# Stick-breaking attention in a hybrid decoder trunk: key sums as matmuls, or as a running sum along the free axis

## The chip, the cores and the metric

The kernel runs on 1 core of one Trainium2 chip. The metric is the device time of one execution in microseconds (us); the time before is the median of three runs.

## The reference

A trunk of two layers works on 512 tokens of width 1024 in fp32: a SwiGLU half-step, a mixer, a cross-attention over 256 memory rows, and a second half-step. The mixer has eight stick-breaking heads of width 64 beside four gated delta-rule heads of width 128, and one output projection over both. The change lies in the stick-breaking heads, for each block of 128 queries:

```python
z = jnp.einsum('bhtd,bhsd->bhts', qb, kb, preferred_element_type=F32) * scale
causal = s_idx < t_idx
log_beta = jax.nn.log_sigmoid(z)
log_1m_beta = jnp.where(causal, log_beta - z, 0.0)
between = lax.cumsum(log_1m_beta, axis=3, reverse=True) - log_1m_beta
a = jnp.where(causal, jnp.exp(log_beta + between), 0.0)
outs.append(jnp.einsum('bhts,bhsd->bhtd', a.astype(v.dtype), vb))
```

With softplus(z) = -log(1 - sigmoid(z)), the weight of key s for query t is exp(z minus the sum of softplus(z) over the keys from s up to t). That sum over the keys is what the change computes in another way. Keys at or after the query get a large negative score.

## The kernel before, in words

Activations lie with features on the 128 partitions and tokens along the free axis. Every fp32 product is made of fp32r parts: an operand is split into a high part (a cast on ACT, `split_act`, L164) and a low part (a subtraction on DVE, `split_low`, L169), and `mm3` (L194) adds three matmuls. All matmuls go through `mm` (L118), transposes through `transpose` (L496). Weights come in units of 128x1024 (`load`, L175, on the SP queue), are split ahead, and `products` (L199) issues eight slices of three matmuls per unit.

TensorE's order is written by hand, the other engines' order is found by the compiler's scheduler. `weave` (L92) runs generators as threads on a virtual clock that counts matmul time: a thread yields a number of virtual ns to wait, or names of marks; whoever comes first in the list and is due goes on. In the mixer (L912) the threads are, in this order: the row norms, the delta-rule heads one after the other (`gdn_head`, L728, with high priority), the four pairs of stick-breaking heads (`sb_pair`, L583), and the projections (`mixer_dense`, L948), which fill the rest. When no thread is due, the virtual clock jumps; the chip waits for data alone.

A delta-rule head (L728 to L903) makes transposes and decays, then five small levels (L809 to L822: a transpose and a mask multiply on DVE, a product, a subtraction), two wide levels (L839 to L850), and a loop over four chunks of three dependent products (L858 to L888). A head's projections need the mark `q` of the head two before; the out-projection's first two pairs of blocks (`project_out`, L449) may begin before the delta-rule heads are done, but wait for the mark `sb3` of the last stick-breaking pair, which is set 17600 virtual ns after its output; then come the turned and gated delta-rule outputs (`gated`, L983).

A stick-breaking pair makes, for each of two heads j: scores (L610) with keys on the partitions, in three groups `SBB` of a PSUM bank each, for key block s all queries from that block on (widths 512, 384, 256 and 128): a mask matmul and two products; softplus from Abs, Exp, Ln on ACT (L621 to L623) and a DVE operation (L624), then a split into two parts. `sums` (L630) subtracts from each score the softplus of all keys behind it, by matmuls with a negative triangle and negative ones (`cr`): for each s and each s2 >= s two matmuls, 20 a head. `weights` (L639) takes the exponential (L642) and splits again; `values` (L645) multiplies by the padded values into bank `av`. L681 copies the result, L683 to L697 norm it.

Of the kernel before, what the change touches and what calls it, by code (L numbers as in the profile page):

```python
# [52 lines left out]
class Trunk:  # L53
# [67 lines left out]
    def setup(self):  # L121
# [23 lines left out]
        self.cr = self.sb([P, 2, P], "cr", F32R)  # L145
        self.cb = self.sb([P, 3, P], "cb", BF16)
        self.ntri, self.nones = (self.cr[:, i, :] for i in range(2))
        self.nsb, self.ngd, self.idb = (self.cb[:, i, :] for i in range(3))
        nc.gpsimd.tensor_copy(self.ntri, stage[:, 0:P])
        nc.gpsimd.tensor_scalar(out=self.nones, in0=self.ones, scalar1=-1.0, scalar2=None, op0=ALU.mult)  # L150
# [430 lines left out]
    SBB = (((2, 0, 256),), ((1, 0, 384), (3, 384, 128)), ((0, 0, 512),))  # L581

    def sb_pair(self, layer, pair):  # L583
        nc = self.nc
        mm = self.mm
        t1s = ("s15", "s16", "s17")
        names = [f"s{i}" for i in range(19, 27)]
# [9 lines left out]
        zs, sp, aa = {}, {}, {}  # L597
        av = None

        def split(t, w):  # L600
            if w <= S // 2:
                one = self.slot(self.turn("sbs", names), F32R)
                hi, lo = one[:, :w], one[:, w:2 * w]
            else:
                hi, lo = (self.slot(self.turn("sbs", names), F32R)[:, :w] for _ in range(2))
            self.split_act(hi, t)
            self.split_low(lo, t, hi)
            return hi, lo

        def scores(j, n):  # L610
            bl = self.SBB[n]
            z = zs[j, n] = self.bank("at", self.AT)
            w = sum(b[2] for b in bl)
            for i, (s, c, width) in enumerate(bl):
                mm(z[:, c:c + P], self.idb, self.nsb, start=i == 0, stop=False, skip_group_check=True)
                ks = slice(s * P, (s + 1) * P)
                mm(z[:, c:c + width], kk[j][:, ks], qq[j][:, s * P:], start=False, stop=False, skip_group_check=True)
                mm(z[:, c:c + width], kk[j][:, ks], ql[j][:, s * P:], start=False, stop=True, skip_group_check=True)
                yield 200.0
            t1 = self.slot(self.turn("t1", t1s))[:, :w]  # L620
            nc.scalar.activation(t1, z[:, :w], AF.Abs)  # L621
            nc.scalar.activation(t1, t1, AF.Exp, scale=-1.0)
            nc.scalar.activation(t1, t1, AF.Ln, bias=1.0)  # L623
            nc.vector.scalar_tensor_tensor(out=t1, in0=z[:, :w], scalar=0.0, in1=t1,  # L624
                                           op0=ALU.max, op1=ALU.add)
            hi, lo = split(t1, w)
            for s, c, width in bl:
                sp[j, s] = (hi[:, c:c + width], lo[:, c:c + width])

        def sums(j, n):  # L630
            bl, z = self.SBB[n], zs[j, n]
            for s, c, width in bl:
                for s2 in range(s, NT):
                    for part in sp[j, s2]:
                        mm(z[:, c + (s2 - s) * P:c + width], self.ntri if s2 == s else self.nones, part,
                           start=False, stop=True, skip_group_check=True)
                    yield 0

        def weights(j, n):  # L639
            w = sum(b[2] for b in self.SBB[n])  # L640
            a = self.slot(self.turn("t1", t1s))[:, :w]
            nc.scalar.activation(a, zs[j, n][:, :w], AF.Exp)  # L642
            aa[j, n] = split(a, w)

        def values(j, n):  # L645
            hi, lo = aa[j, n]
            for i, (s, c, width) in enumerate(self.SBB[n]):
# [10 lines left out]
        for j in range(2):  # L658
# [11 lines left out]
            if j == 0:  # L670
                yield from scores(1, 1)
# [596 lines left out]
```

## Time and profile before

| | |
|---|---|
| median of 3 runs | 2524.72 us (2523.73 to 2525.19) |
| profiled execution | 2528.47 us |
| its span, first to last instruction | 2526.7 us |
| mean granted TensorE clock | 0.996 of full speed |
| layer 0's mixer, from its first projection to its last block | about 365 to 740 us |
| layer 1's mixer | about 1620 to 2000 us |

Rows give engine, line, operation, output<-inputs by the program's names, shapes and how often. PE is TensorE, PEld its weight loads, DVE VectorE, ACT ScalarE, POOL GpSimd. Timelines give start and duration in us; a burst is merged into one row with its count, and its duration ends with the modelled end of its last matmul, which overlaps the next row. In brackets stands idle time of the engine before the row and what ended it.

### The profile page before, as it was taken

How to read it: one execution, taken by the hardware profiler on the slowest of the kernel's cores; microseconds unless marked ns; L12 is line 12 of the kernel's file. 1: busy time of each engine (PE TensorE's matmuls, PEld its weight loads, DVE VectorE, ACT ScalarE, POOL GpSimd, SP SyncE). 2: the span in 40 equal slices, each digit the busy share in tenths (PEclk: the TensorE clock that was granted, in tenths of full speed). 3: DMA queues.
4: the chain of work that ended last, by engine and by line, in shares of the span. 5: the costliest groups of instructions: out<-in, count | busy, mean ns of one | idle time of the engine just before them, and what ended most of it. 6: DMA issues, size and time to landing. Idle time of an engine off the chain costs nothing.

```text
span 2526.7 us, 30844 instructions
## 1 busy us (share of the span) xinstructions
PE 2469.2 (98%) x12268; PEld 2070.6 (82%) x12268; DVE 1438.3 (57%) x2585; ACT 970.7 (38%) x1545; POOL 10.5 (0%) x21
## 2 busy tenths in 40 slices
PE   8999999999999999999999999999999999999997
PEld 6888887888889888888888888778888988888886
DVE  6443467788675563444554443687876755544345
ACT  4222236555544432222322222466555444322222
POOL 0000000000000000000000000000000000000000
PEclk9999999999999999999999999999999999999999
DMA  5223232111233123332323222311111432322322
GB/s 192 84 100 100 98 94 67 42 51 36 66 110 125 59 92 100 100 101 88 101 95 98 97 89 94 98 59 42 51 43 51 150 101 67 100 85 99 100 94 65
DMA packets 64672, 220.16 MB, mean 87 GB/s; under 512 B 7312, under 2 KB 9616, under 8 KB 64528
## 3 DMA queue, kind: packets, MB, share of 16 engines
q1 hardware_dynamic: 64096, 217.15, 26.5%
q8 instruction: 96, 1.57, 0.3%
q10 hardware_dynamic: 432, 1.04, 0.1%
q14 instruction: 48, 0.39, 0.0%
HBM read 216.07 MB, written 2.10 MB: 86 GB/s over the span
## 4 chain that ended last, share of the span: by engine, by line
PE 89%; DVE 8%; ACT 1%; issue 1%; DMA 0%; DVEq 0%; SPq 0%; ACTq 0%
PE b L118 88%; DVE wlo L169 2%; PE b L496 1%; DVE s L169 1%; ACT whi L164 1%; DVE qkv L713 1%; DVE s L624 0%; DVE s L810 0%; DVE qk L169 0%; DMA wraw<-f1i 0%; DVE s L822 0%; ACT s L164 0%; DVE s L835 0%; DVE s L836 0%; DVE s L429 0%
## 5 line engine op out<-in xcount | busy, mean ns | idle before, releaser
L118 PE MATMUL b<-xh,whi 128*128 128x512 f32 x2112 | 843.6, 399 | 10.1 <-ACT whi L164 8.4
L118 PE MATMUL b<-xh,wlo 128*128 128x512 f32 x2112 | 826.3, 391 | 0.0
L118 PE MATMUL b<-xl,whi 128*128 128x512 f32 x2112 | 825.7, 391 | 0.2
L164 ACT CAST whi<-wraw 128x1024 fp32r<-128x1024 f32 (+1 forms) x408 | 407.9, 1033 | 1033.5 <-PE b L118 947.6
L118 PE MATMUL b<-s,whi 128*128 128x512 f32 (+1 forms) x2136 | 591.6, 364 | 0.2 <-ACT whi L164 0.2
L169 DVE TENSOR_TENSOR wlo<-wraw,whi 128x1024 fp32r<-128x1024 f32 (+1 forms) x408 | 479.3, 1200 | 72.2 <-ACT whi L164 72.0
L118 PEld LDWEIGHTS b<-xh,whi 128*128 128x128 f32 x2112 | 398.7, 189 | 88.7 <-ACT whi L164 8.4
L118 PEld LDWEIGHTS b<-xh,wlo 128*128 128x128 f32 x2112 | 397.6, 188 | 84.8 <-DVE wlo L169 0.8
L118 PEld LDWEIGHTS b<-xl,whi 128*128 128x128 f32 x2112 | 398.6, 189 | 79.2 <-DVE xl L169 1.5
L118 PEld LDWEIGHTS b<-s,whi 128*128 128x128 f32 x2136 | 382.3, 188 | 64.5 <-issue 0.6
L118 PE MATMUL b<-s,wlo 128*128 128x512 f32 (+1 forms) x1068 | 387.1, 362 | 0.0
L352 DVE TENSOR_TENSOR s<-b,rb 128x512 f32<-128x512 f32 x88 | 60.7, 691 | 450.6 <-PE b L118 450.5
L118 PEld LDWEIGHTS b<-s,wlo 128*128 128x128 f32 x1068 | 201.2, 188 | 32.3
L364 DVE TENSOR_TENSOR s<-b,rb 128x512 f32<-128x512 f32 (+1 forms) x98 | 66.3, 680 | 224.8 <-PE b L118 224.7
L164 ACT CAST s<-s 128x512 fp32r<-128x512 f32 x186 | 107.4, 579 | 158.9 <-DVE s L355 124.6
L169 DVE TENSOR_TENSOR s<-s,s 128x512 fp32r<-128x512 f32 x186 | 118.3, 637 | 65.6 <-ACT s L164 65.2
L118 PEld LDWEIGHTS b<-s,s 128*128 128x128 f32 x656 | 84.6, 191 | 13.1 <-issue 8.1
L118 PE MATMUL b<-s,s 128*128 128x128 f32 (+2 forms) x656 | 86.7, 274 | 3.5 <-DVE rqt L224 1.8
L365 DVE SCALAR_TENSOR_TENSOR h<-s,h 128x512 f32<-128x512 f32 (+1 forms) x98 | 63.0, 673 | 0.0
L353 ACT ACTIVATE s<-s 128x512 f32<-128x512 f32 x88 | 54.9, 625 | 17.6 <-DVE s L352 17.6
L118 PE MATMUL b<-s,cr 128*128 128x128 f32 (+3 forms) x320 | 55.1, 311 | 6.6 <-DVE s L169 6.6
L355 DVE TENSOR_TENSOR s<-b,s 128x512 f32<-128x512 f32 x88 | 60.1, 684 | 1.6 <-ACT s L353 1.4
(240 smaller groups left out, 1820.3 us busy)
## 6 DMA issues: line engine op xcount, KB each, us to landing
wraw<-f1i SPq DMA_DIRECT2D x88, 512.0 KB, 3.7
wraw<-f2i SPq DMA_DIRECT2D x88, 512.0 KB, 3.7
wraw<-wi SPq DMA_DIRECT2D x56, 512.0 KB, 3.5
wraw<-f1o SPq DMA_DIRECT2D x32, 512.0 KB, 3.8
wraw<-xkv SPq DMA_DIRECT2D x32, 512.0 KB, 3.5
wraw<-f2o SPq DMA_DIRECT2D x32, 512.0 KB, 4.2
wraw<-wo SPq DMA_DIRECT2D x16, 512.0 KB, 3.5
wraw<-xq SPq DMA_DIRECT2D x16, 512.0 KB, 3.5
```

What stands on the lines that cost most here:

```text
L118: self.nc.tensor.matmul(out, lhsT, rhs, **kw)
L164: self.nc.scalar.copy(hi, src)
L169: self.nc.vector.tensor_tensor(lo, src, hi.bitcast(F32), op=ALU.subtract)
L352: nc.vector.tensor_tensor(gt, ps[0], self.rb, op=ALU.mult)
L353: nc.scalar.activation(gt, gt, AF.Silu)
L355: nc.vector.tensor_tensor(m, ps[1], gt, op=ALU.mult)
L364: nc.vector.tensor_tensor(t, p, self.rb[:, cols], op=ALU.mult)
L365: nc.vector.scalar_tensor_tensor(out=h, in0=t, scalar=0.5, in1=h, op0=ALU.mult, op1=ALU.add)
L496: self.nc.tensor.transpose(out, src, self.ident[:src.shape[0], :src.shape[0]])
L713: nc.vector.scalar_tensor_tensor(out=y, in0=cv[:, 1 + i:1 + i + S], scalar=w[i], in1=y, op0=ALU.mult, op1=ALU.add)
```

## The change: what it does

Scores are computed with queries on the partitions and keys along the free axis. Query block t takes its own t + 1 key blocks (widths 128 to 512), in groups `SBQ`. After softplus, DVE makes a running sum along the keys, from the last key backwards (`tensor_tensor_scan` with a reversed access), one per query block; the sum is subtracted from the score in PSUM and ACT takes the exponential in place. The sums' matmuls, the first splits and the constants `ntri` and `nones` go. Ten transposes of 128x128 a head bring the weights to keys on the partitions, into three PSUM banks laid out by `SBK`; they are split from there, and the value products stay. Each head now waits 11000 virtual ns ahead of its transposes, 2200 after the splits and 500 between value blocks, in place of 1700 a head, 800 and 2600. The running sums take slots s19 to s21, the split weights s22 to s26.

```diff
--- before.py
+++ after.py
@@ -142,12 +142,8 @@
         self.bones = c[:, C_BO:C_BO + 2]
         stage = self.slot("s0")
         nc.scalar.dma_start(stage[:, :3 * P], self.a["csr"])
-        self.cr = self.sb([P, 2, P], "cr", F32R)
         self.cb = self.sb([P, 3, P], "cb", BF16)
-        self.ntri, self.nones = (self.cr[:, i, :] for i in range(2))
         self.nsb, self.ngd, self.idb = (self.cb[:, i, :] for i in range(3))
-        nc.gpsimd.tensor_copy(self.ntri, stage[:, 0:P])
-        nc.gpsimd.tensor_scalar(out=self.nones, in0=self.ones, scalar1=-1.0, scalar2=None, op0=ALU.mult)
         nc.gpsimd.tensor_copy(self.nsb, stage[:, P:2 * P])
         nc.gpsimd.tensor_copy(self.ngd, stage[:, 2 * P:3 * P])
         nc.gpsimd.tensor_copy(self.idb, self.ident)
@@ -578,13 +574,17 @@
         self.mark(f"sbp{pair}", 2600.0)
 
 
-    SBB = (((2, 0, 256),), ((1, 0, 384), (3, 384, 128)), ((0, 0, 512),))
+    SBQ = (((3, 0, 512),), ((2, 0, 384), (0, 384, 128)), ((1, 0, 256),))
+
+    SBK = ((0, 0), (1, 0), (2, 0), (1, 384))
 
     def sb_pair(self, layer, pair):
+
+
         nc = self.nc
         mm = self.mm
         t1s = ("s15", "s16", "s17")
-        names = [f"s{i}" for i in range(19, 27)]
+        names = [f"s{i}" for i in range(22, 27)]
         yield (f"sbp{pair}",)
         b = self.bank("av", self.AV)
         self.transposes(b, self.vf)
@@ -594,89 +594,77 @@
         self.split_low(lo, src, hi)
         self.mark(f"vt{pair}")
         kk, qq, ql = self.qk[pair]
-        zs, sp, aa = {}, {}, {}
+        raw, aa = {}, {}
         av = None
 
-        def split(t, w):
+        def scores(j, n):
+            bl = self.SBQ[n]
+            z = self.bank("at", self.AT)
+            w = sum(b[2] for b in bl)
+            for i, (t, c, width) in enumerate(bl):
+                mm(z[:, c + width - P:c + width], self.nsb, self.idb, start=i == 0, stop=False, skip_group_check=True)
+                ts = slice(t * P, (t + 1) * P)
+                mm(z[:, c:c + width], qq[j][:, ts], kk[j][:, :width], start=False, stop=False, skip_group_check=True)
+                mm(z[:, c:c + width], ql[j][:, ts], kk[j][:, :width], start=False, stop=True, skip_group_check=True)
+                yield 200.0
+            t1 = raw[n] = self.slot(self.turn("t1", t1s))[:, :w]
+            nc.scalar.activation(t1, z[:, :w], AF.Abs)
+            nc.scalar.activation(t1, t1, AF.Exp, scale=-1.0)
+            nc.scalar.activation(t1, t1, AF.Ln, bias=1.0)
+            nc.vector.scalar_tensor_tensor(out=t1, in0=z[:, :w], scalar=0.0, in1=t1,
+                                           op0=ALU.max, op1=ALU.add)
+            run = self.slot(self.turn("run", ("s19", "s20", "s21")))
+            for t, c, width in bl:
+                back = slice(c + width - 1, c - 1 if c else None, -1)
+                nc.vector.tensor_tensor_scan(out=run[:, back], data0=self.ones[:, 0:1].to_broadcast([P, width]),
+                                             data1=t1[:, back], initial=0.0, op0=ALU.mult, op1=ALU.add)
+            nc.vector.tensor_tensor(t1, z[:, :w], run[:, :w], op=ALU.subtract)
+            nc.scalar.activation(t1, t1, AF.Exp)
+
+        def turned(n, at):
+            for t, c, width in self.SBQ[n]:
+                for s in range(t + 1):
+                    i, c2 = self.SBK[s]
+                    c2 += (t - s) * P
+                    self.transpose(at[i][:, c2:c2 + P], raw[n][:, c + s * P:c + (s + 1) * P])
+
+        def weights(n, at):
+            w = sum(b[2] for b in self.SBQ[n])
             if w <= S // 2:
                 one = self.slot(self.turn("sbs", names), F32R)
                 hi, lo = one[:, :w], one[:, w:2 * w]
             else:
                 hi, lo = (self.slot(self.turn("sbs", names), F32R)[:, :w] for _ in range(2))
-            self.split_act(hi, t)
-            self.split_low(lo, t, hi)
-            return hi, lo
-
-        def scores(j, n):
-            bl = self.SBB[n]
-            z = zs[j, n] = self.bank("at", self.AT)
-            w = sum(b[2] for b in bl)
-            for i, (s, c, width) in enumerate(bl):
-                mm(z[:, c:c + P], self.idb, self.nsb, start=i == 0, stop=False, skip_group_check=True)
-                ks = slice(s * P, (s + 1) * P)
-                mm(z[:, c:c + width], kk[j][:, ks], qq[j][:, s * P:], start=False, stop=False, skip_group_check=True)
-                mm(z[:, c:c + width], kk[j][:, ks], ql[j][:, s * P:], start=False, stop=True, skip_group_check=True)
-                yield 200.0
-            t1 = self.slot(self.turn("t1", t1s))[:, :w]
-            nc.scalar.activation(t1, z[:, :w], AF.Abs)
-            nc.scalar.activation(t1, t1, AF.Exp, scale=-1.0)
-            nc.scalar.activation(t1, t1, AF.Ln, bias=1.0)
-            nc.vector.scalar_tensor_tensor(out=t1, in0=z[:, :w], scalar=0.0, in1=t1,
-                                           op0=ALU.max, op1=ALU.add)
-            hi, lo = split(t1, w)
-            for s, c, width in bl:
-                sp[j, s] = (hi[:, c:c + width], lo[:, c:c + width])
-
-        def sums(j, n):
-            bl, z = self.SBB[n], zs[j, n]
-            for s, c, width in bl:
-                for s2 in range(s, NT):
-                    for part in sp[j, s2]:
-                        mm(z[:, c + (s2 - s) * P:c + width], self.ntri if s2 == s else self.nones, part,
-                           start=False, stop=True, skip_group_check=True)
-                    yield 0
-
-        def weights(j, n):
-            w = sum(b[2] for b in self.SBB[n])
-            a = self.slot(self.turn("t1", t1s))[:, :w]
-            nc.scalar.activation(a, zs[j, n][:, :w], AF.Exp)
-            aa[j, n] = split(a, w)
-
-        def values(j, n):
-            hi, lo = aa[j, n]
-            for i, (s, c, width) in enumerate(self.SBB[n]):
-                vs = slice(64 * j, 64 * j + P)
-                self.mm3(av[:, s * P:], (self.vpad[0][:, s, vs], self.vpad[1][:, s, vs]),
-                         (hi[:, c:c + width], lo[:, c:c + width]),
-                         j == 0 and n == 0 and i == 0, True, skip=True)
-                yield 0
+            self.split_act(hi, at[n][:, :w])
+            self.split_low(lo, at[n][:, :w], hi)
+            aa[n] = hi, lo
+
+        def values(j, s):
+            n, c = self.SBK[s]
+            cs = slice(c, c + S - s * P)
+            vs = slice(64 * j, 64 * j + P)
+            self.mm3(av[:, s * P:], (self.vpad[0][:, s, vs], self.vpad[1][:, s, vs]),
+                     (aa[n][0][:, cs], aa[n][1][:, cs]), j == 0 and s == 0, True, skip=True)
 
         for n in range(3):
             yield from scores(0, n)
             yield 0
         av = self.bank("av", self.AV)
         for j in range(2):
-            yield 1700.0
+            yield 11000.0
+            at = [self.bank("at", self.AT) for _ in range(3)]
             for n in range(3):
-                yield from sums(j, n)
-                if n < 2:
-                    weights(j, n)
-                    yield 0
-            if j == 0:
-                yield from scores(1, 0)
-                yield 800.0
-            yield from values(j, 0)
-            weights(j, 2)
-            if j == 0:
-                yield from scores(1, 1)
-            yield 0
-            yield from values(j, 1)
-            yield 0
-            if j == 0:
-                yield from scores(1, 2)
-                self.mark(f"qk{pair}")
-                yield 2600.0
-            yield from values(j, 2)
+                turned(n, at)
+            for n in range(3):
+                weights(n, at)
+            yield 2200.0
+            for s in range(NT):
+                if j == 0 and s < 3:
+                    yield from scores(1, s)
+                    if s == 2:
+                        self.mark(f"qk{pair}")
+                values(j, s)
+                yield 500.0 if s < 3 else 0
         o = self.slot(("s0", "s1", "s13", "s37")[pair])
         nc.scalar.copy(o, av)
         sq = self.slot(self.turn("t1", t1s))
```

## Rows read from the trace of the kernel before

**Rows 1.** The page, first line and part 1: busy time, share, instructions.
```profile
span 2526.7 us, 30844 instructions
...
PE 2469.2 (98%) x12268; PEld 2070.6 (82%) x12268; DVE 1438.3 (57%) x2585; ACT 970.7 (38%) x1545; POOL 10.5 (0%) x21
```

**Rows 2.** Busy time by stretch: us; PE, PEld, DVE, ACT, POOL; PEclk, DMA, GB/s.
```profile
481.00:551.00 70.00, 66.20 (x403) 57.13 (x402) 57.23 (x150) 39.73 (x81) 0.00 (x0) 1.00 0.14 46
```

**Rows 3.** Timeline of PE: first transposes of two delta-rule heads (start, us).
```profile
480.97 0.60 PE L496 MATMUL b<-cst,qkv 128*128 128x128 f32 x4
...
551.40 0.60 PE L496 MATMUL b<-cst,qkv 128*128 128x128 f32 x4
```

**Rows 4.** Timeline of PE: the end of layer 0's mixer.
```profile
676.53 0.38 PE L118 MATMUL b<-s,s 128*128 128x128 f32 x2
...
692.37 0.38 PE L118 MATMUL b<-rhs,s 128*128 128x128 f32 x2
...
693.13 0.49 PE L118 MATMUL b<-yv,s 128*128 128x128 f32 x2 [0.38 <-DVE yv L870]
...
700.51 1.04 PE L496 MATMUL b<-cst,s 128*128 128x128 f32 x8
```

**Rows 5.** Matmuls that read the triangle and ones: ns min/median/max, first and last start, forms.
```profile
L118 PE MATMUL b<-s,cr x320: 219/281/663, 430.1 to 1917.1; 128*128 128x128 f32 x64, 128*128 128x256 f32 x48, 128*128 128x384 f32 x32, 128*128 128x512 f32 x16
```

**Rows 6.** Timeline of PE: one stick-breaking head's sums and what follows each burst.
```profile
522.51 1.68 PE L118 MATMUL b<-s,cr 128*128 128x256 f32 x12
524.02 1.11 PE L118 MATMUL b<-s,s 128*128 128x128 f32 x8
524.88 1.07 PE L118 MATMUL b<-s,cr 128*128 128x512 f32 x4
525.79 1.05 PE L118 MATMUL b<-s,s 128*128 128x128 f32 x8
526.60 0.65 PE L118 MATMUL b<-s,cr 128*128 128x256 f32 x4
527.09 0.45 PE L118 MATMUL b<-s,vph 128*128 128x256 f32 x2
```

**Rows 7.** Timeline of PE: four transposes.
```profile
543.62 0.60 PE L496 MATMUL b<-cst,s 128*128 128x128 f32 x4
```

**Rows 8.** Groups by shape, layer 0's mixer: DVE and ACT, count, busy us, mean ns.
```profile
L169 DVE TENSOR_TENSOR s<-s,s 128x512 fp32r<-128x512 f32 x32 | 21.8, 682 | 3.9 <-ACT s L164 3.9
...
L164 ACT CAST s<-s 128x512 fp32r<-128x512 f32 x32 | 19.7, 616 | 9.6 <-PE b L118 9.4
...
L169 DVE TENSOR_TENSOR s<-s,s 128x256 fp32r<-128x256 f32 x16 | 6.7, 421 | 1.1 <-ACT s L164 1.0
...
L850 DVE TENSOR_TENSOR s<-s,b 128x512 f32<-128x512 f32 x8 | 5.5, 688 | 11.1 <-PE b L118 11.1
```

**Rows 9.** Timelines of ACT and DVE: one stick-breaking pair.
```profile
494.90 0.39 ACT L621 ACTIVATE s<-b 128x256 f32<-128x256 f32 x1
...
505.48 0.68 DVE L169 TENSOR_TENSOR s<-s,s 128x512 fp32r<-128x512 f32 x1
...
531.13 0.58 ACT L681 COPY s<-b 128x512 f32<-128x512 f32 x1 [2.20 <-PE b L118]
```

**Rows 10.** Busy time by stretch, as rows 2: first part of a head.
```profile
481.00:502.00 21.00, 18.86 (x108) 15.37 (x106) 18.45 (x60) 13.60 (x34) 0.00 (x0) 1.00 0.16 51
502.00:523.00 21.00, 20.26 (x131) 17.95 (x131) 19.29 (x47) 11.87 (x23) 0.00 (x0) 1.00 0.16 50
```

**Rows 11.** Timelines of DVE and PE: a level of a delta-rule head.
```profile
512.56 0.69 DVE L810 TENSOR_TENSOR s<-s,cst 128x512 f32<-128x512 f32 x1
...
513.99 1.00 PE L118 MATMUL b<-s,s 128*128 128x64 f32 x8
```

**Rows 12.** Busy time by stretch, as rows 2: a fall of the granted clock.
```profile
640.00:644.00 4.00, 3.21 (x18) 2.68 (x18) 3.96 (x8) 3.86 (x8) 0.00 (x0) 1.00 0.00 0
644.00:648.00 4.00, 4.00 (x27) 3.82 (x26) 3.82 (x12) 1.59 (x3) 0.00 (x0) 0.72 0.19 37
```

## The prediction

> **What bounds the kernel now.** The page comes first: TensorE is busy for 98% of the span, DVE for 57%, ACT for 38%, GpSimd for 10.5 us in all [rows 1]. So the question is what the change does to TensorE's instruction stream; shares of the other engines matter only where they make TensorE wait. The change touches the two mixers (365 to 704 us, and again in layer 1), so next comes the table of busy time for one delta-rule head there: TensorE 66.2 of 70 us, DVE 57.2, ACT 39.7 [rows 2]. DVE is at 82% in the mixer, not 57%: the engine that receives work is the second-busiest just there.
>
> What sets the mixer's length? Its threads are woven by a virtual clock; the delta-rule thread has the first turn, the stick-breaking thread the second, and projections fill what is left. A delta-rule head starts right behind the one before, at 480.97 and 551.40, 70.4 us apart [rows 3]. Its length comes from its own waits (the yields), not from how much other work there is: others only fill its gaps. In layer 0 that filling lasts almost exactly to the end. The last head's chunk loop runs from 676.5 to 693.6 between projection matmuls, after it come out-projection matmuls that were held back for the last stick-breaking pair, and the turned gates follow at 700.5 [rows 4]. I read this as a schedule in which TensorE's work and the delta-rule chain end together: taking away filler there shortens only one of the two.
>
> **What goes from TensorE.** The sums: 20 matmuls per head, 16 heads, 320 in all [rows 5]. One head's take 1.51 + 0.91 + 0.49 = 2.91 us, each from the start of a burst to the start of what follows it (522.51 to 524.02, 524.88 to 525.79, 526.60 to 527.09) [rows 6].
>
> **What comes.** Ten 128x128 transposes per head (1+2+3+4 blocks). A burst of eight lasts 1.04 us [rows 4] and one of four 0.60 us [rows 7], so one more costs 0.11 us and ten cost 1.08 us with the shorter spacing of the streams. Scores and values keep their matmuls: scores swap stationary and moving operand, with the same four widths (128 to 512) and four bias matmuls. Net: 16 x (2.91 - 1.08) = **-29.3 us** of TensorE work, 14.6 us per layer.
>
> **What moves between DVE and ACT.** Per head ACT loses three casts (0.62 us at 512 columns) [rows 8]; ACT isn't the limit, I count nothing. DVE loses three low-part subtractions of the sums (0.68, 0.68, 0.42) and gains three subtractions of the running sum from PSUM (0.69 at 512 columns), which cancel; the low parts of the weights stay, read from PSUM at the same price [rows 8]. What is really added are four running sums per head (512, 384, 256 and 128 columns). No such row exists. Lower end: an elementwise operation, 0.42 us for 256 and 0.68 for 512 columns [rows 8], so 0.16 us + 1.02 ns a column: 0.69 + 0.55 + 0.42 + 0.29 = 1.95 us a head. Upper end: a running sum is serial, each element needs the one before; at two element times a column it is 1.21 + 0.94 + 0.68 + 0.42 = 3.25 us. I take the lower end, as all rows of DVE of this size lie on that line, and keep the upper for the range. Two heads of this kind share a delta-rule period: DVE goes from 57.2 to between 61 and 64 us of 70.
>
> [...]
>
> Two setup operations of GpSimd go; that engine works 10.5 us in the whole kernel [rows 1], and its cover is everything before the mixer: nothing. No DMA is added. Weight loads move earlier with the projections, at 46 GB/s in this stretch [rows 2]: nothing.
>
> **What is lost again.**
>
> (a) The end of each mixer. With 14.6 us less filler the projections run dry that much earlier, about where the last head's chunk loop begins. TensorE then meets its real dependences: the chunk's step from one product to the next takes 0.76 us when nothing lies between (692.37 to 693.13) [rows 4]. Eleven steps make 8.4 us where the filled loop took 17: 8.6 us are won, 14.6 - 8.6 = 6.0 us of TensorE idle remain, 12 us for two layers. Bounds: 0 if the chain follows the shorter work completely, 9 us a layer if the last stick-breaking pair ends last. That pair's chain grows: a pair now runs from its first score at 494.9 to its output copy at 531.1 [rows 9], 36 us; the yields grow from 6.8 to 29.4 us, TensorE's part falls 3.7, so 55 us, which fits a period of 70.4 but brings the last pair close to the end.
>
> (b) Waits on a fuller DVE. The first 42 us of a period hold 18.45 + 19.29 us of DVE work [rows 10], 4.3 us are free, and most of the added work falls there. The delta-rule levels are tight: DVE ends a mask multiply at 513.25 and TensorE needs it at 513.99 [rows 11], room for about one 0.69 us operation. DVE is in order, so an operation that comes to lie in front stalls TensorE with everything queued behind. Six such steps a head (four levels, two opening products), half of them behind one further operation of 0.69 us that is on average half done: 6 x 0.5 x 0.34 = 1.0 us a head, 8 us for eight. Bounds: -0.5 us a head (the old sums' own waits go) to 3.6 (below).
>
> [...]
>
> (d) The new 11 us wait before the transposes. In the old chain the last low part starts at 505.5, 10.6 us after the first activation at 494.9 [rows 9]; the new chain has a running sum and an exponential where cast and low part were, at most 1.3 us more for a group, and its 11 us count only from the third group's scores on. That fits, so nothing; if it didn't, TensorE would stand with projections and delta-rule work queued behind the transpose.
>
> Sum: -29.3 + 12 + 8 + 3 = **-6.3 us**. The profiled execution took 2528.5 us around its span of 2526.7 [rows 1], 3.8 above the median of the runs; I put the difference on the median, 2524.7 - 6.3 = 2518 us.
>
> **Rivals.**
> - TensorE bounds throughout and the chains give way: all 29.3 us come, 2495 us. For it: 98% busy. Against it: head starts tied to head ends [rows 3] and the even finish [rows 4]. Chance 0.14.
> - DVE becomes the limit of the first 42 us of each head. If running sums go at two element times, 6.5 us press into 4.3 free, and a tight step meets half of a 1.2 us operation: 6 x 0.6 = 3.6 us a head, 29 us in all; -29.3 + 12 + 29 + 3 = +15, 2539 us, slower. It decides from 1.8 us of stall a head on, (29.3 - 12 - 3) / 8. For it: 18.45 and 19.29 of 21 us busy [rows 10]; against: ACT is relieved and weight splits can slip. Chance 0.24. [...]
> - A draw, stalls of 1.2 to 2.4 us a head: 2520 to 2530 us. Chance 0.18.
> - My forecast, part of the saving kept: 0.44, of which a little lies within the bound.
>
> A measurement of this kernel can tell about 0.2%, 5 us, from no change. Faster by more: 0.14 + 0.39 = 0.53; within: 0.18 + 0.03 = 0.21; slower: 0.26, the DVE rival with a late last pair. The range reaches from -27 us (the near half of the full saving) to +16: 2498 to 2541. The likeliest case alone spans 2505 to 2521.
>
> **What would show it.** No matmul reads the constants' tile any more; 160 transposes more; running sums on DVE of 0.69 us (lower end) or 1.2 (upper) at 512 columns. Head starts still 70 to 73 us apart: the chain paces. If they close to 67, the full-saving rival is right. [...] I am wrong if the last head's chunk loop is still filled, or if transposes wait long for the exponential.

## The result and the profile after

The changed kernel takes **2556.97 us** (median of 4 runs, 2556.38 to 2563.07), the kernel before, run beside it, 2524.22 (2523.7 to 2525.19): ratio **1.0135**, interval 1.0117 to 1.0152. The forecast was 2518 in 2498 to 2541; the sign was wrong. The profiled execution has a span 27.9 us longer than before at a granted clock of 0.985 instead of 0.996.

The first line and part 1 of the page of after answer to [rows 1]:

```profile
span 2554.6 us, 30493 instructions
...
PE 2466.0 (97%) x12108; PEld 2056.1 (80%) x12108; DVE 1474.5 (58%) x2649; ACT 946.2 (37%) x1497; POOL 8.3 (0%) x19
```

TensorE has 160 instructions fewer, as forecast (320 matmuls gone, 160 transposes new), yet it is hardly less busy: part of what is left ran at about half the granted clock (0.50 and 0.54 in stretches below). The four running sums, groups of DVE by shape in layer 0's mixer (count, then busy us and mean ns):

```profile
L619 DVE TENSOR_TENSOR_SCAN s<-cst,s 128x512 f32<-128x512 f32 x8 | 9.8, 1222 | 0.1
L619 DVE TENSOR_TENSOR_SCAN s<-cst,s 128x384 f32<-128x384 f32 x8 | 7.6, 948 | 0.0
L619 DVE TENSOR_TENSOR_SCAN s<-cst,s 128x256 f32<-128x256 f32 x8 | 5.5, 683 | 0.0
L619 DVE TENSOR_TENSOR_SCAN s<-cst,s 128x128 f32<-128x128 f32 x8 | 3.3, 407 | 0.0
```

They add up to 3.26 us a head, the upper end: 2.1 ns more for each column, where an elementwise operation takes 1.02 [rows 8].

**Where the time went.** Busy time by stretch of after, one row for each delta-rule head of layer 0 (columns as rows 2):

```profile
365.00:480.50 115.50, 109.53 (x588) 89.28 (x587) 95.88 (x205) 68.24 (x115) 0.53 (x1) 1.00 0.21 69
480.50:553.30 72.80, 65.17 (x378) 55.29 (x377) 63.01 (x160) 37.72 (x75) 0.00 (x0) 0.95 0.16 51
553.30:628.40 75.10, 70.41 (x400) 58.95 (x400) 61.50 (x159) 36.99 (x76) 0.00 (x0) 0.95 0.12 43
628.40:714.50 86.10, 72.49 (x399) 60.13 (x398) 59.00 (x176) 37.56 (x82) 0.52 (x1) 0.90 0.12 37
```

The last of these stretches in the kernel before, and the first operation on the turned gates, before (L989) and after (L977):

```profile
621.80:701.10 79.30, 75.27 (x437) 64.54 (x436) 55.77 (x158) 42.86 (x88) 0.52 (x1) 0.98 0.17 54
...
701.15 1.41 DVE L989 SCALAR_TENSOR_TENSOR s<-b,gn,qk 128x512 f32<-128x512 f32 x2 [3.07 <-PE b L496]
...
714.55 1.41 DVE L977 SCALAR_TENSOR_TENSOR s<-b,gn,qk 128x512 f32<-128x512 f32 x2 [8.55 <-PE b L492]
```

The second head begins when it did before (480.55; 480.97 in [rows 3]). The next two are 72.8 and 75.1 us long instead of 70.4, and the last one with the tail to the turned gates takes 86.1 us where it took 79.3. The gates come at 714.55 instead of 701.15, 13.4 us late in layer 0 and 28.2 in both layers together (1977.51 against 1949.34): the whole loss, and the 29.3 us of saved work with it, lie in the mixers. DVE has more to do in a head, as forecast (63.0 and 61.5 us where [rows 2] have 57.2), and the clock, 1.00 in [rows 2] and 0.98 in the last stretch of before, is 0.95 to 0.90.

What paces the mixer now? The timeline of ACT points at the stick-breaking pairs: L611 is a pair's first activation on its scores, L669 the copy of its output.

```profile
422.06 0.60 ACT L611 ACTIVATE s<-b 128x512 f32<-128x512 f32 x1
...
482.68 0.62 ACT L669 COPY s<-b 128x512 f32<-128x512 f32 x1
...
503.00 0.60 ACT L611 ACTIVATE s<-b 128x512 f32<-128x512 f32 x1 [0.48 <-PE b L118]
...
576.22 0.60 ACT L611 ACTIVATE s<-b 128x512 f32<-128x512 f32 x1 [0.27 <-PE b L118]
...
650.48 0.60 ACT L611 ACTIVATE s<-b 128x512 f32<-128x512 f32 x1
```

And in the kernel before: the last operation of the second pair's norm (L697), and the last pair's first activation (L621).

```profile
544.26 0.75 DVE L697 SCALAR_TENSOR_TENSOR s<-s,gn,b 128x512 f32<-128x512 f32 x1 [0.74 <-PE b L496]
...
635.80 0.39 ACT L621 ACTIVATE s<-b 128x256 f32<-128x256 f32 x1
```

From first score to output copy the first pair takes 60.6 us (forecast: 55), the next two 57.0 and 59.1. But the thread is not done there: the RMS norm of the output follows (sums, a square root in small operations, transposes, two yields), whose last operation, L685, starts at 499.48. Only then does the next pair start. So the pairs stand 81, 73 and 74 us apart, more than the 70.4 of a delta-rule head, where in the kernel before they stood 71, 70 and 70 apart; the last one starts 14.7 us late (650.48 against 635.80), about as late as the gates. The output copies of the first two pairs came at 460.68 and 531.13 before, ahead of the next head's start; here they come at 482.68 and 559.98, behind it (480.55 and 553.36), and the norm falls into the opening of that head, where DVE has 18 of 21 us to do [rows 10]. The timeline of DVE and PE there:

```profile
489.35 0.16 DVE L676 TENSOR_SCALAR sms<-b 128x8 f32<-128x8 f32 x1
...
495.27 0.16 DVE L222 SCALAR_TENSOR_TENSOR sny<-snt,sny 128x8 f32<-128x8 f32 x1
495.35 0.75 DVE L701 SCALAR_TENSOR_TENSOR qkv<-cv,gn,qkv 128x512 f32<-128x512 f32 x1
496.01 0.16 DVE L220 TENSOR_TENSOR snt<-sny 128x8 f32<-128x8 f32 x1
496.13 0.75 DVE L701 SCALAR_TENSOR_TENSOR qkv<-cv,gn,qkv 128x512 f32<-128x512 f32 x1
...
497.78 0.43 DVE L680 COPY s<-sny 128x512 f32<-128x512 f32 x1
498.35 1.09 PE L492 MATMUL b<-cst,s 128*128 128x128 f32 x4 [3.98 <-DVE s L680]
...
499.48 0.75 DVE L685 SCALAR_TENSOR_TENSOR s<-s,gn,b 128x512 f32<-128x512 f32 x1 [1.27 <-PE b L492]
```

Each small step of the square root (sn.., 0.16 us) needs the one before, and from the sixth step on operations of the other threads, 0.2 to 1.2 us each, slip in between. This string of small steps takes from 489.35 to 498.2, and TensorE stands 3.98 us at the transposes behind it. Busy time by stretch, same place:

```profile
490.00:494.00 4.00, 4.00 (x24) 3.41 (x22) 3.86 (x15) 1.67 (x2) 0.00 (x0) 1.00 0.00 0
494.00:498.00 4.00, 0.37 (x2) 0.00 (x0) 3.97 (x10) 0.11 (x1) 0.00 (x0) 0.87 0.42 131
498.00:502.00 4.00, 3.65 (x18) 3.62 (x19) 1.81 (x5) 0.07 (x1) 0.00 (x0) 0.50 0.00 0
502.00:506.00 4.00, 4.00 (x17) 2.89 (x18) 2.25 (x4) 2.79 (x5) 0.00 (x0) 0.78 0.01 4
```

After it stood, TensorE works at a granted clock of 0.50 for 4 us and of 0.78 in the 4 us after that, where it had 1.00 ahead of the stall: by an estimate from these rows, the stall of 4 us costs some 3 more (4 x 0.50 + 4 x 0.22 = 2.9). The two largest waits of PE between 365 and 760 us (us in total, times, longest):

```profile
PE b L492 <- DVE s L680: 11.3, 4, 4.0
PE b L118 <- DVE yv L858: 3.1, 5, 1.0
```

The two largest of the kernel before, which has no wait at these transposes:

```profile
PE b L118 <- DVE s L771: 4.9, 3, 1.7
PE b L118 <- DVE s L169: 4.4, 9, 0.8
```

At the end of the mixer it is the last pair that ends last. Timeline of PE:

```profile
687.72 0.77 PE L118 MATMUL b<-rhs,s 128*128 128x128 f32 x2 [0.54 <-DVE rhs L852]
...
691.49 0.77 PE L118 MATMUL b<-rhs,s 128*128 128x128 f32 x2 [0.54 <-DVE rhs L852]
...
697.19 0.28 PE L118 MATMUL b<-s,vpl 128*128 128x128 f32 x1
...
698.81 1.05 PE L118 MATMUL b<-cst,s 128*128 128x2 f32 x8 [1.34 <-ACT s L671]
...
702.68 1.09 PE L492 MATMUL b<-cst,s 128*128 128x128 f32 x4 [2.82 <-DVE s L680]
...
713.92 1.03 PE L492 MATMUL b<-cst,s 128*128 128x128 f32 x8
```

The last chunks, the last values, the sums of the norm and its transposes come one after the other with little between them; in the kernel before, out-projections filled this place up to 700 [rows 4]. The same stretch by busy time:

```profile
684.00:692.00 8.00, 5.89 (x22) 4.91 (x23) 3.63 (x10) 4.09 (x14) 0.00 (x0) 0.54 0.06 24
...
700.00:708.00 8.00, 3.75 (x10) 2.56 (x11) 3.63 (x15) 0.62 (x1) 0.52 (x1) 0.61 0.01 2
```

**A balance.** All waits of TensorE in the two mixers sum to 34.4 us before and 64.3 after (365 to 760 and 1620 to 2060 us); the clock lost, (0.996 - 0.985) x 2554.6, is 28 us, and as both clocks are rounded to a thousandth, 25 to 31. Work -29.3, waits +29.9, clock +28.1: +28.7, where the spans differ by 27.9.

### The profile page after: what moved, and what is told of

Same layout as the page of the kernel before. It is cut to its first block, busy times and chain, and to the rows that moved or that the text cites. A ratio compares the mean times of both kernels' runs of the same rounds, so it can differ in the third digit from the quotient of the medians.

```text
span 2554.6 us, 30493 instructions
## 1 busy us (share of the span) xinstructions
PE 2466.0 (97%) x12108; PEld 2056.1 (80%) x12108; DVE 1474.5 (58%) x2649; ACT 946.2 (37%) x1497; POOL 8.3 (0%) x19
## 4 chain that ended last, share of the span: by engine, by line
PE 86%; DVE 11%; ACT 2%; issue 1%; DMA 0%; DVEq 0%; ACTq 0%
PE b L118 84%; DVE wlo L165 2%; PE b L492 2%; DVE qkv L701 1%; DVE s L619 1%; DVE s L165 1%; DVE s L798 1%; DVE s L614 0%; DVE s L621 0%; ACT whi L160 0%; DMA wraw<-f1i 0%; DVE s L829 0%; DVE s L810 0%; DVE s L797 0%; DVE cv L696 0%
## 5 line engine op out<-in xcount | busy, mean ns | idle before, releaser
L160 ACT CAST whi<-wraw 128x1024 fp32r<-128x1024 f32 (+1 forms) x408 | 407.9, 1033 | 1054.6 <-PE b L118 970.0
L160 ACT CAST s<-s 128x512 fp32r<-128x512 f32 x90 | 55.1, 613 | 125.2 <-DVE s L351 124.6
L165 DVE TENSOR_TENSOR s<-s,s 128x512 fp32r<-128x512 f32 x90 | 61.2, 682 | 56.6 <-ACT s L160 56.4
L492 PE MATMUL b<-cst,s 128*128 128x128 f32 (+1 forms) x360 | 56.4, 292 | 27.3 <-DVE s L680 22.6
L165 DVE TENSOR_TENSOR s<-b,s 128x512 fp32r<-128x512 f32 (+1 forms) x92 | 56.4, 638 | 35.2 <-ACT s L160 35.0
L492 PEld LDWEIGHTS b<-cst,s 128*128 128x128 f32 (+1 forms) x360 | 45.2, 152 | 36.5 <-issue 25.8
L160 ACT CAST s<-b 128x512 fp32r<-128x512 f32 (+1 forms) x92 | 46.5, 552 | 62.5 <-PE b L492 39.6
```

Of the source, the lines that this page charges most:

```text
L160: self.nc.scalar.copy(hi, src)
L165: self.nc.vector.tensor_tensor(lo, src, hi.bitcast(F32), op=ALU.subtract)
L492: self.nc.tensor.transpose(out, src, self.ident[:src.shape[0], :src.shape[0]])
```

## Experiments

All runs in one table: edit, median, ratio to the kernel before with interval, clock, TensorE's waits in the two mixers, and the balance (work + waits + clock, against before) beside the difference of the spans. Clock, waits, balance and spans are those of the profiled execution, which lies within 4 us of the median but for e10 (2569.2, 12 above), e7 (6 above) and e3 (5 below).

| run | edit | us | ratio, 95% | clock | waits | balance | spans |
|---|---|---|---|---|---|---|---|
| after | | 2556.97 | 1.0117-1.0152 | .985 | 64.3 | +28.7 | +27.9 |
| e1 | before, long waits | 2578.11 | 1.0193-1.0227 | .982 | 63.3 | +65.0 | +53.6 |
| e2 | after, wait 7 | **2510.72** | 0.9930-0.9959 | .993 | 37.2 | -19.0 | -15.8 |
| e3 | after, no sums | 2547.64 | 1.0073-1.0110 | .987 | 54.6 | +13.8 | +14.1 |
| e16 | e2, no sums | 2498.91 | 0.9880-0.9910 | .993 | 26.4 | -29.8 | -29.3 |
| e4 | before, spare sums | 2535.44 | 1.0027-1.0057 | .995 | 42.1 | +10.2 | +8.6 |
| e7 | after, wait 5 | 2529.70 | 1.0011-1.0030 | .987 | 46.1 | +5.2 | +7.6 |
| e12 | after, wait 6 | 2528.43 | 1.0004-1.0023 | .992 | 51.1 | -2.5 | -0.1 |
| e15 | after, wait 8 | 2542.99 | 1.0054-1.0084 | .989 | 59.7 | +13.8 | +15.8 |
| e8 | after, wait 9 | 2541.25 | 1.0049-1.0079 | .991 | 57.8 | +6.8 | +10.8 |
| e17 | before, norm later | 2534.30 | 1.0021-1.0049 | .994 | 37.5 | +8.2 | +5.6 |
| e5 | norm in 1st wait | 2568.96 | 1.0160-1.0190 | .983 | 73.0 | +42.7 | +39.9 |
| e6 | e5, wait 7 | 2556.26 | 1.0107-1.0141 | .983 | 64.1 | +33.6 | +26.6 |
| e18 | norm in 2nd wait | 2556.82 | 1.0105-1.0135 | .985 | 63.6 | +28.0 | +28.0 |
| e9 | norm longer | 2565.43 | 1.0148-1.0178 | .981 | 67.3 | +42.1 | +37.7 |
| e14 | last pair short | 2564.41 | 1.0141-1.0171 | .982 | 67.1 | +39.3 | +38.7 |
| e10 | norm first on DVE | 2557.15 | 1.0113-1.0147 | .981 | 65.8 | +40.6 | +40.7 |
| e11 | e10, wait 7 | 2515.47 | 0.9948-0.9977 | .992 | 36.8 | -16.8 | -13.0 |
| e13 | norm not awaited | 2546.66 | 1.0066-1.0100 | .985 | 53.2 | +17.5 | +19.2 |

The balance closes within about 4 us, but for e1 (11) and e6 (7). It is an account, not a cause: the clock falls where TensorE stands (0.50, then 0.78 behind the 3.98 us above), so one stall appears in both terms.

### Which part of the change loses?

**e1_before_long_waits**: the kernel before with waits as long as the change's, all its matmuls as they were.

```diff
-            yield 1700.0
+            yield 13000.0
```

> The kernel before with its two waits of 1.7 us raised to 13 us, so that a stick-breaking pair waits as long by the virtual clock as in the changed kernel; all work as before. Theory A (the chain of the four pairs, one after the other, has become the longest in the mixer and ends last): pairs with their norms some 75 us apart, the last pair's output behind the delta-rule heads, 10 to 14 us more per layer, 2544 to 2554 us in all. Theory B (the added running sums overload DVE and TensorE waits for it): DVE's work is unchanged, so 2520 to 2530 us.

**e2_after_short_wait**: the changed kernel, wait for the transposes shortened.

```diff
-            yield 11000.0
+            yield 7000.0
```

> The changed kernel with its wait of 11 us cut to 7 us. Theory A: 8 us less per pair, up to 32 us off the chain of a mixer, which is then no longer the longest: 2525 to 2542 us. Theory B: DVE work is the same and the transposes now come before their data, so waits move there: 2550 us or more.

Measured 2578.11 and 2510.72. The waits alone cost the kernel before 53 us, more than either theory gave. The first wait of PE in e1's first mixer is at the norm's transposes (L692 is the copy that they read):

```profile
PE b L496 <- DVE s L692: 14.0, 4, 5.3
```

With as much in the second mixer, that is 28.0 of the 28.9 us by which its waits rise (63.3 - 34.4), though it has all its old matmuls and no running sums. In the changed kernel, four us less of virtual time in each wait give 46 us back, more than expected, and **this version beats both kernels** (ratio 0.9944, interval 0.9930 to 0.9959). So the loss sits in where the wait puts the instructions that follow it; at this length the change is a gain. In the timeline of DVE and PE of e2 the same norm's string begins ahead of the next head's first transposes (478.36), and only operations as short as its own lie between:

```profile
477.73 0.15 DVE L676 TENSOR_SCALAR sms<-b 128x8 f32<-128x8 f32 x1
...
480.34 0.17 DVE L222 SCALAR_TENSOR_TENSOR sny<-snt,sny 128x8 f32<-128x8 f32 x1
...
480.57 0.42 DVE L680 COPY s<-sny 128x512 f32<-128x512 f32 x1
...
481.13 0.63 PE L492 MATMUL b<-cst,s 128*128 128x128 f32 x4
```

It takes 3.3 us here (477.73 to 480.99) and 8.9 in after, and the transposes behind it don't wait. The longest waits of PE in e2's first mixer are others, and short:

```profile
PE b L118 <- DVE s L759: 3.6, 3, 1.7
PE b L118 <- DVE s L798: 3.4, 5, 0.8
```

**e3_after_no_sums** and **e16_short_wait_no_sums**: the running sums left out, at 11 and at 7 us. **e4_before_spare_sums**: running sums that nobody reads, added to the kernel before.

```diff
-            run = self.slot(self.turn("run", ("s19", "s20", "s21")))
-            for t, c, width in bl:
...
-            nc.vector.tensor_tensor(t1, z[:, :w], run[:, :w], op=ALU.subtract)
+            nc.vector.tensor_tensor(t1, z[:, :w], t1, op=ALU.subtract)
```

> The changed kernel without its running sums: each score has only its own softplus subtracted, so what the sum over the keys would compute is left out; all waits stay. 6.5 us less DVE work per delta-rule head. Theory A: the chain's waits are by the virtual clock and stay; small gains where TensorE waited for DVE, 2540 to 2555 us. Theory B: most of the loss goes, 2500 to 2525 us.

```diff
-            yield 11000.0
+            yield 7000.0
...
-            nc.vector.tensor_tensor(t1, z[:, :w], run[:, :w], op=ALU.subtract)
+            nc.vector.tensor_tensor(t1, z[:, :w], t1, op=ALU.subtract)
```

> The run with 7 us without its running sums (the sum over the keys is left out). 6.5 us of DVE work less per delta-rule head. If the running sums still cost TensorE waits there, as they did in the kernel before (10.6 us): 2496 to 2505 us. If DVE has room at this wait: 2507 to 2514 us.

```diff
+            for i in range(2 if w < S else 3):
+                nc.vector.tensor_tensor_scan(out=self.spare, data0=self.ones[:, 0:1].to_broadcast([P, P]),
+                                             data1=t1[:, i * P:(i + 1) * P][:, ::-1], initial=0.0, op0=ALU.mult, op1=ALU.add)
...
             hi, lo = split(t1, w)
```

> The kernel before with eight running sums of 128 columns per stick-breaking head into a tile that nobody reads: 8 x 0.41 = 3.3 us of DVE a head, the same load as in the changed kernel, without its waits, transposes or missing matmuls. Theory A: DVE has room or the sums' waits grow a little, 2524 to 2534 us. Theory B: the delta-rule steps wait behind the sums, 2540 us or more.

The sums' price is measured three times: 9.3 us at a wait of 11 (2556.97 - 2547.64; the executions of e3 spread over 2543 to 2554), 11.8 at 7 (2510.72 - 2498.91) and some 11 in the kernel before (2535.44 against 2524.88 beside it; e4 lies between its two branches). That is a fifth of the 57 us that lie between the saved work and the result (-29.3 to +27.9). e3 still has 54.6 us of waits, and the one at the norm's transposes is as long without the sums as in after (first mixer; L675 is the copy there):

```profile
PE b L492 <- DVE s L675: 11.3, 4, 4.0
```

e16 also shows the work term whole: its waits are 8.0 us fewer than before (26.4 against 34.4), the lost clock is 7.5 us, the two about cancel, and the span is 29.3 us shorter.

### How long may the wait be?

Each is the edit of e2 with another number: **e7_after_wait5**, **e8_after_wait9**, **e12_after_wait6**, **e15_after_wait8**.

```diff
-            yield 11000.0
+            yield 5000.0
```

> The changed kernel with a wait of 5 us in place of 11. The chain from the last score to the weights takes 8 us or more in the changed kernel's trace, so transposes stand and TensorE with them: 3 us for each of 16 heads over the run with 7 us, 2515 to 2555 us. If the data come in time nevertheless: 2500 to 2512 us.

```diff
-            yield 11000.0
+            yield 9000.0
```

> The changed kernel with a wait of 9 us. Theory A: each us of wait counts eight times a layer as long as the chain is the longest (16 us of time per us of wait in all, at most), so between the runs with 7 and 11 us: 2520 to 2540 us; a step to either side would mean that one late event decides, not the length.

```diff
-            yield 11000.0
+            yield 6000.0
```

> A wait of 6 us in place of 11, between the runs with 5 us (2530) and 7 us (2511). If the optimum is set by when the weights' data come, it lies between: 2510 to 2525 us. Under 2508 us the optimum would lie below 7 us.

```diff
-            yield 11000.0
+            yield 8000.0
```

> A wait of 8 us. Between the runs with 7 (2511) and 9 us (2541). By length alone half way, 2520 to 2532 us. Near 2511 or under it, the optimum is broad and the run with 6 us the odd one; near 2541, the run with 7 us owes its time to a lucky order.

From 5 to 9 and 11 us: 2530, 2528, 2511, 2543, 2541, 2557. The rise with the wait is there, but 7 us lies some 25 us below a line through its neighbours (2528 and 2543): its time is that of one order of instructions that happens to fit, no optimum of a smooth curve. The runs with 6 and 9 us came out above their ranges, the one with 8 us where it was to show a lucky order at 7. What stands changes with the number. In e8 the wait at the norm's transposes is not the largest; the first wait of PE in its first mixer is for low parts, above all of the stick-breaking weights, whose bank the next scores need:

```profile
PE b L118 <- DVE s L165: 10.3, 6, 3.9
```

### Is it the norm?

Theory: the pair with its norm is too long for the period, or the norm lies in the wrong place. **e17_before_norm_later** puts the norm of the first three pairs off by 15 us in the kernel before.

```diff
-        yield 4900.0
+        yield 4900.0 if pair == 3 else 20000.0
```

> The kernel before with the norm of the first three pairs put off by 15 us (its first wait 20 us in place of 4.9), into a time in which the stick-breaking thread only waits for the next projections; the last pair's is left. The norm now falls from the calm end of a delta-rule head into the full opening of the next. Length theory: the thread has that slack, 2524 to 2532 us. Phase theory (what costs is in which part of a delta-rule head the norm's small DVE operations fall): TensorE stands several us at each of its transposes and its clock falls, 2535 to 2555 us.

2534.3, 9 us slower. The wait of after appears in the kernel before, in its waits of PE in the first mixer:

```profile
PE b L496 <- DVE s L692: 6.8, 3, 3.4
```

So a norm in the full opening makes TensorE stand at its transposes without any other part of the change. But 9 us are a small part of the 53 that the long waits cost this kernel (e1): these 13.5 us of both mixers raise the sum of all waits by only 3.1 (37.5 against 34.4), as others get shorter.

**e5_after_norm_beside** lets the norm of a pair run within the first wait of the next pair; **e6_both** does so at 7 us; **e18_after_norm_in_second_wait** within the second wait, on the delta-rule thread's PSUM bank.

```diff
+            if j == 0 and pair:
+                yield from self.left
+                yield 1400.0
+            else:
+                yield 11000.0
...
+        self.left = self.sb_norm(layer, pair, o, sq)
+        if pair == 3:
+            yield from self.left
```

> The changed kernel with its 11 us waits, but each pair's norm (two waits of 4.9 and 4.7 us) done inside the first wait of the next pair in place of ahead of it; only the last pair's norm stays at the end. Theory A: 13 to 17 us less per pair, so the chain is about 60 us a pair and no longer the longest, though the last pair still comes late by its own length: 2510 to 2530 us. If instead it is the waits on DVE at the norm's copy alone that cost (11.3 us a layer), they move with it: 2535 us or more.

```diff
...
+                yield from self.left
+                yield 0
+            else:
+                yield 7000.0
```

> Both: a wait of 7 us, and the norm inside the next pair's first wait. Theory A: the chain has slack already at 7 us, so nothing or little more than the short wait alone: 2505 to 2514 us. If the chain still ends last with the short wait: 2490 to 2503 us.

```diff
+            if j and pair:
+                yield from self.left
+                yield 3800.0
+            else:
+                yield 11000.0
...
+        b = self.bank("gd", self.GD)
```

> The changed kernel with its 11 us waits and the norm beside, as in the run with the norm inside the next pair's first wait (2569), but inside the next pair's second wait, in the calm part of a delta-rule head, with a bank of the delta-rule heads. Phase theory: the standing at the norm's transposes goes and the thread is shorter, 2515 to 2540 us. If the norm beside costs wherever it stands: 2555 us or more.

2568.96, 2556.26 and 2556.82: none brings the gain that a shorter thread or a calmer place would give. e5 and e18 lie in their other branches, e6 in neither. In e5 the norm's transposes wait longer than in after (waits of PE, first mixer):

```profile
PE b L492 <- DVE s L691: 15.5, 3, 8.7
```

**e9_after_long_norm** lengthens the norm, **e14_after_last_pair_short** shortens the last pair alone.

```diff
-        yield 4700.0
+        yield 9500.0
```

> The changed kernel, all waits as they are, but 9.5 us in place of 4.7 between the norm's column sums and its transposes. Theory A (the length of the chain): each pair 4.8 us longer, 2570 to 2600 us. Theory N (TensorE stands at the norm's transposes, 11.3 us a layer, because its string of small DVE operations now falls where DVE is full, and its clock halves behind): the standing goes, 2530 to 2545 us.

```diff
-            yield 11000.0
+            yield 7000.0 if pair == 3 else 11000.0
```

> The changed kernel with its wait cut from 11 to 7 us in the last of the four pairs alone. Length theory (the mixer ends some 11 us after the last pair's normed output, whatever comes before): 8 us less per layer, 2537 to 2546 us, the turned gates at about 706 us. If the cost lies in the first three pairs (standing and the clock in the middle of the mixer): 2550 to 2558 us.

e9 costs 8 us, less than length alone would, more than place alone; e14, where the last pair should have ended earlier, is 7 us slower than after, outside both branches. Its last pair is no shorter for 8 us less of virtual time: 49.0 us from the cast of its values (L160) to its output copy (651.41 to 700.42), and 47.6 in after (649.91 to 697.51). That fits the rule of the order that the virtual clock jumps where no thread is due: at the end of the mixer little is left to fill a wait with. Length isn't the cause by itself.

**e10_after_norm_first** gives the norm's DVE operations priority in the order of instructions, **e11_short_wait_norm_first** the same at 7 us; **e13_after_norm_unread** lets the transposes read another tile, so that they need not wait for the string.

```diff
+        with self.tc.high_priority():
+            nc.vector.tensor_scalar(out=ms, in0=b[:, 0:8], scalar1=1.0 / 64, scalar2=EPS,
...
```

> The changed kernel with its 11 us wait, the norm's DVE operations (the mean square, the rsqrt steps, the copy that the transposes read) put ahead in DVE's order. Theory A: the chain's waits stay, the last pair still ends last, 2545 to 2557 us. Theory N: the 22.6 us that TensorE stands at these transposes in both layers go, with the clock behind them, 2518 to 2538 us.

```diff
-            yield 11000.0
+            yield 7000.0
...
+        with self.tc.high_priority():
```

> The wait of 7 us with the norm's operations put ahead. The run with 7 us shows no wait over 0.5 us at the norm, so both theories: 2503 to 2514 us, and a delta-rule head that is delayed by it would show as more than 2514.

```diff
-        self.transposes(b, wide)
+        self.transposes(b, sq)
```

> The changed kernel, all waits and operations kept, but the norm's transposes read the squares in place of the copied rsqrt, so the norm's factor is left out of the result and TensorE need not wait for the string of small DVE operations. Standing theory: 11.3 us a layer less standing, and the clock that halves behind it, 2522 to 2535 us. If the standing only moves to the next dependence (as with the norm put ahead): 2545 to 2560 us.

e10 gains nothing, e11 lies 5 us above e2, hardly more than the intervals leave open, and e13 gains 10 where the theory of standing wanted 22 or more; it lies in its other branch. In e10 the first pair's string does get shorter, 4.3 us (493.07 to 497.41), and its transposes don't wait; TensorE stands at the next ones, which bring in the next pair's values, because they write the one bank `av` that the norm's last operation (L686 there) still reads:

```profile
504.07 1.09 PE L492 MATMUL b<-cst,s 128*128 128x128 f32 x4 [4.04 <-DVE s L686]
```

In e13 the same transposes of the next pair wait for the same operation (waits of PE, first mixer):

```profile
PE b L492 <- DVE s L685: 6.3, 3, 3.6
```

**What stays open.** Shown: the length of the wait alone decides between a gain of 14 us (7 us) and a loss of 33 (11 us), the long waits cost the kernel before 53 us without the rest of the change, and the loss arrives as standing TensorE with the lower clock behind it (0.50 behind a stall of 3.98 us). Not settled: which of the places of standing is first cause. The norm's transposes are the longest (22.6 us in after), but without their wait only 10 us come back (e13). Take away one (e10, e13, e18) and another comes. That the pairs' period of 73 to 81 us against 70.4 is the root is argued from the timeline alone; e5 and e14 speak against it as the only cause, and so does e15: its pairs start 72.3, 71.0 and 71.2 us apart, nearly as in the kernel before, and it takes 2543. Not tested: the kernel before with waits a little longer or shorter than its 1.7 us, so whether its own order is as lucky as that of 7 us is open.

## Why the prediction was wrong, point by point

- **The work, -29.3: right.** 160 instructions fewer, and e16's span is 29.3 us shorter once the sums are out and the wait is 7 us.
- **The running sums: the wrong end.** 1.22 us at 512 columns, not 0.69; the lower end was taken because the elementwise rows lay nearest. A recurrence is not the kind of operation that those rows show; the prediction had the upper end too, as an estimate of twice the elementwise time a column. The 2.1 ns beside 1.02 [rows 8] bear out the factor; why it is two, no run shows.
- **(b) the fuller DVE, 8 us: near in size** (9 to 12), in part by luck: it was worked out with the lower end of the sums, and no run shows that its price is paid in the levels; that operations which lie in front on DVE make TensorE stand is measured at the norm's transposes, up to 3.98 us a time in after.
- **The step that failed is (d) with the pair's length in (a)**: "55 us, which fits a period of 70.4", and "That fits, so nothing". The copy of the output was taken as the pair's end. The thread goes on through the norm for some 17 us more (482.68 to 499.48), which before lay ahead of the head's full opening; 60.6 + 17 don't fit. The trace of before had a sign of it: from the copy at 531.13 to the norm's last operation at 544.26 are 13.1 us, and 55 and 13.1 leave 2.3 of the 70.4. And (d) asked only whether the data would be ready at the transposes, not what the longer wait would move behind itself; it put that term at nothing. The waits alone cost the kernel before 53 us (e1). TensorE does not wait long for the exponential, as said; its longest waits are for the norm, 28.0 us in e1 and 22.6 in after, none before. How much of the loss begins there stays open, as said above.
- **(a) the dry end, 12 us in two layers**: the last pair ends last, the bound named there. The last head and its tail take 6.8 us more than before (86.1 - 79.3), with 14.6 us less work in the layer. The dry loop itself was priced at 0.76 us a step, 2.3 for the three steps of a chunk; at 0.54 of the clock a chunk takes 3.8 us (687.72 to 691.49).
- **The clock: 3 in the sum, 25 to 31 lost.** No run shows the term of 3. What the runs show in its place is a granted clock of 0.50 and 0.78 behind a stall of 3.98 us, 0.54 and 0.61 where the mixer runs out of work, and 0.90 over the last stretch of layer 0's mixer, which had 0.98 before: an estimate of 7 us more lost there alone (86.1 x 0.10 - 79.3 x 0.02). The stalls ahead of these falls were not foreseen, neither in number nor in length.
- **The rivals.** That DVE becomes the limit (2539) came nearest in sign: the running sum takes 2.1 ns a column, two element times of 1.02, and waits rose by 29.9 us, about its 29. But the sums make a fifth of what was lost, so that the two numbers agree is luck, and the longest standing is at the norm's transposes, as long without the sums (e3), not in the levels. The full saving failed, and so did the draw.

## What to carry to other kernels

Follow a hand-woven thread to its last step before you compare its length with a period; what counts is when the next round can start. When a wait grows in an order written by hand, list every later part of that thread and look up what it will now lie beside: a string of small dependent operations is cheap among others as short (3.3 us) and dear among long ones (8.9 us). Price a TensorE stall with the clock behind it (here some 3 us for a stall of 3.98, by the estimate above), and try a few lengths of a new wait before the change is judged; here the same change at 7 us is a gain of 0.6%, at 11 us a loss of 1.35%, and 6 and 8 us gain nothing.

## What was not expected of the hardware

The running sum took 2.1 ns a column and 0.14 us beside ((1222 - 407) / 384 columns; 407 - 128 x 2.12 = 136 ns), twice the 1.02 ns a column of an elementwise operation [rows 8]. And standing cost TensorE again afterwards: granted clock 0.50 and 0.78 in the two stretches of 4 us after a stall of 3.98, and 0.54 and 0.61 in two stretches of 8 us where the mixer ran out of work and TensorE was busy 5.89 and 3.75 us.
